# Fourier tables of the convolution made in pieces during the first eight steps, and adaLN sums on VectorE issued at half the rate

## Chip, core and metric

The kernel runs on one core of a Trainium2 chip. The metric is the device time of one execution in microseconds; the median of three runs of the kernel before is 1817.89 us (1816.94 to 1818.36).

A core has five engines that each work through a list of their own, in order: TensorE (PE; its weight loads are PEld), VectorE (DVE), ScalarE (ACT), GpSimd (POOL) and SyncE (SP), which here issues nearly all loads from memory. An instruction that waits holds up everything behind it on its engine.

## What is computed

Two layers over 256 latent tokens with a context prefix of 256 tokens, width 1024. Layer 0 mixes tokens with a Conformer convolution, layer 1 with a bidirectional chunkwise mLSTM; each is followed by a squared-ReLU MLP. Six adaLN vectors for each layer and stream modulate and gate the sub-layers.

```python
for i in range(DEPTH):                                   # DEPTH = 2
    sh1, sc1, g1, sh2, sc2, g2 = adaln(c[:, None, :], ada_w[i], ada_b[i])     # silu(c) @ w + b
    csh1, csc1, cg1, csh2, csc2, cg2 = adaln(c_ctx, ada_w[i], ada_b[i])
    u, uc = modulate(h, sh1, sc1), modulate(hc, csh1, csc1)
    y, yc = conformer_conv(...) if i % 2 == 0 else mlstm_mixer(...)
    h = layer_norm(ALPHA * h + g1 * y, ...)
    h = layer_norm(ALPHA * h + g2 * sq_relu_mlp(modulate(h, sh2, sc2), w1, w2), ...)
    ...                                                  # hc the same, while it is needed

def conformer_conv(u, rows, ...):
    a = u @ w_pw1 + b_pw1
    a = a[..., :CONV_DIM] * sigmoid(a[..., CONV_DIM:])
    a = dwconv(a, w_dw)                                  # 31 taps for each channel
    a = silu(layer_norm(a + b_dw, ln_g, ln_b))
    return a @ w_pw2 + b_pw2
```

## The kernel before

Activations lie with channels on the 128 partitions and the 512 tokens (256 context, 256 latent) along the free axis. Every large product is made in float32 accuracy from three products of rounded parts: `mm3` multiplies the high parts (L177), high with low (L180) and low with high (L181). A weight block comes as a 1 MB load into `raw` (three buffers) and is split by ScalarE into `wh` (L154) and by VectorE into `wl` (L155), four buffers each.

**The first eight steps** (loop over `f`, `start0`, `start1`, `start2`). Step f loads a block of adaLN weights, one of the input and one of the first projection. TensorE makes the adaLN product into the PSUM bank `fl` (L291), VectorE copies it (L603), TensorE folds it (L299, bank `ln`), VectorE adds the bias (L608, L609), ScalarE and VectorE make the modulated input `u` in two parts (L574, L575, L577), and TensorE adds its share to four output blocks of the first projection (`start2`, twelve products of 512 columns). TensorE's products of this loop are held in the order of the program.

**The tables.** The convolution over time is made with Fourier tables of length 128: F0, G1, G2 (transform and back) and WC, WS. VectorE makes them by a cosine polynomial (L654 to L671), which stands behind the eight steps in the program. WC and WS times the 31 taps give the taps' spectrum `Hc`, `Hs` (four products of TensorE at L693 with 31 rows, in float32, read by ScalarE at L694). It is first needed in `spectral` (L762 on), after the projection's eighth output block.

**The adaLN sums on VectorE.** Nine of the adaLN units of layer 1 are not made as products with a thin operand but as sums: `AdaV.step` loads one 256 KB block into `ar` (one buffer, on SP's queue, L353) and adds it times a column to two accumulators of 128x512 (L357 first, L359 after). Eight steps are a unit. Then `rows()` sums over the partitions with a product by ones (L372) into a PSUM tile that ScalarE copies (L374), and after each second unit `end()` transposes the rows (L381) into another tile, to which VectorE adds the bias (L382). `ada_n1` is four units beside the MLP of layer 0, `ada_n2` five more: two are made beside the v projection, and the other three (24 steps) here:

- `queries(h)`, four heads: eight weight blocks of `wq` each, with one `ada_n2.step()` after each block;
- `pair(p)`, two pairs of heads: after the queries of both heads, 16 output blocks m, each with 24 products of 272 columns into the bank `mm`, read by ScalarE and VectorE into `rr` (L154, L155, L1164), and, one block later, 12 products of 512 columns into the four accumulators `acc`, which take the banks `ln`, `ln`, `cv` and `fl`.

PSUM has eight banks: `mm` three, rotating through all large products, `ln` two, `cv` two, `fl` one. `rows()` and `end()` take `fl`, the bank that `acc` takes as well.

The order of each engine's list is made by the framework's scheduler from the program; it is fixed when the kernel is built.

Of the kernel before, what the change touches and what calls it, by code (L numbers as in the profile page):

```python
# [72 lines left out]
def hybrid_kernel(ctx: ExitStack, tc: tile.TileContext, xT, vecs_d, wdw_d, ada0_w, ada_w, wg_d, pw1a, pw1, pw2, w1_0, w2_0,  # L73
# [28 lines left out]
    def psum(tag="mm"):  # L102
        return pp.tile([P, 512], F32, tag=tag, name=nm(tag), bufs={"mm": 3, "ln": 2, "fl": 1, "cv": 2}[tag])
# [237 lines left out]
    class AdaV:  # L341
# [22 lines left out]
                self.end()  # L364

        def rows(self, n):
            ps = psum("fl")
            if n == 0:
                self.sb = tmp("F")
            for s in range(2):  # L370
                j = 32 * (2 * n + s)
                nc.tensor.matmul(ps[j:j + 32, :], ones[:, 0:32], self.acc[s], start=True, stop=True,  # L372
                                 tile_position=(0, j))
            nc.scalar.copy(self.sb[64 * n:64 * n + 64], ps[64 * n:64 * n + 64])  # L374

        def end(self):
            nu, o = self.nu, _OFF[f"ada_b{self.l}"][0] + 4 * self.u0
            r = 64 * nu
            tr = psum("fl")[:, 0:4 * r]
            for b in range(4):  # L380
                nc.tensor.transpose(tr[:, b * r:(b + 1) * r], self.sb[:r, b * P:(b + 1) * P], ident[:r, :r])  # L381
            nc.vector.tensor_tensor(  # L382
                ada[self.l][:, 4 * self.u0:4 * (self.u0 + nu), :].rearrange("p (v b) s -> p b v s", b=4),
                tr.rearrange("p (b v s r) -> p b v s r", b=4, v=nu, s=2)[:, :, :, :, 0],
                vecs[:, o:o + 4 * nu].rearrange("p (v b o) -> p b v o", b=4, o=1).broadcast_to([P, 4, nu, 2]), op=ALU.add)
# [241 lines left out]
    pin[0] = False

    HL = L // 2
    ij = F()
    fj, jj = ij[:, 0:L], ij[:, L:2 * L]
    pc = padp.tile([P, 8], F32, name="pc")
    exact = dict(channel_multiplier=0, allow_small_or_imprecise_dtypes=True)
    nc.gpsimd.iota(fj[:, 0:HL + 1], [[1, HL + 1]], base=0, **exact)
    nc.gpsimd.iota(fj[:, HL + 1:L], [[1, HL - 1]], base=1, **exact)
    nc.gpsimd.iota(jj, [[1, L]], base=0, **exact)
    p_, gt, fp, p15, ph1, ph2, cf, z0 = [pc[:, i:i + 1] for i in range(8)]  # L640
    nc.gpsimd.iota(p_, [[1, 1]], base=0, channel_multiplier=1, allow_small_or_imprecise_dtypes=True)
    nc.vector.tensor_scalar(gt, p_, float(HL), None, op0=ALU.is_gt)
    nc.vector.scalar_tensor_tensor(fp, gt, -float(HL), p_, op0=ALU.mult, op1=ALU.add)
    nc.vector.tensor_scalar(p15, p_, float(NTAP // 2), None, op0=ALU.subtract)
    nc.vector.tensor_scalar(ph1, gt, -L / 4, None, op0=ALU.mult)
    nc.vector.tensor_scalar(ph2, gt, -L / 4, L / 4, op0=ALU.mult, op1=ALU.add)

    nc.vector.tensor_scalar(z0, p_, 0.0, None, op0=ALU.is_equal)
    nc.vector.tensor_scalar(cf, p_, float(HL), None, op0=ALU.is_equal)
    nc.vector.tensor_tensor(cf, cf, z0, op=ALU.add)  # L650
    nc.vector.tensor_scalar(cf, cf, -1.0 / L, 2.0 / L, op0=ALU.mult, op1=ALU.add)
    tab = padp.tile([P, 5 * L], F32, name="tab")
    F0, G1, G2, WC, WS = [tab[:, i * L:(i + 1) * L] for i in range(5)]
    nc.vector.tensor_scalar(F0, fj, p_, None, op0=ALU.mult)  # L654
    nc.vector.tensor_scalar(G1, jj, fp, ph1, op0=ALU.mult, op1=ALU.add)
    nc.vector.tensor_scalar(G2, jj, fp, ph2, op0=ALU.mult, op1=ALU.add)
    nc.vector.tensor_scalar(WC, fj, p15, None, op0=ALU.mult)
    nc.vector.tensor_scalar(WS, fj, p15, -L / 4, op0=ALU.mult, op1=ALU.add)
    nc.vector.tensor_scalar(F0[:, HL + 1:L], F0[:, HL + 1:L], -L / 4, None, op0=ALU.add)
    for t_ in (tab[:, 0:3 * L], tab[:, 3 * L:5 * L]):  # L660
        tz, sq_ = [F()[:, :t_.shape[-1]] for _ in range(2)]
        nc.vector.tensor_scalar(tz, t_, 1.0 / L, MAGIC, op0=ALU.mult, op1=ALU.add)
        nc.vector.tensor_scalar(tz, tz, MAGIC, -float(L), op0=ALU.subtract, op1=ALU.mult)
        nc.vector.tensor_tensor(t_, t_, tz, op=ALU.add)
        nc.vector.scalar_tensor_tensor(tz, t_, -1.0, t_, op0=ALU.mult, op1=ALU.max)
        nc.vector.tensor_scalar(t_, tz, -1.0, L / 4, op0=ALU.mult, op1=ALU.add)
        nc.vector.tensor_tensor(sq_, t_, t_, op=ALU.mult)
        nc.vector.tensor_scalar(tz, sq_, SIN[5], None, op0=ALU.mult)
        for k in (4, 3, 2, 1):
            nc.vector.scalar_tensor_tensor(tz, tz, SIN[k], sq_, op0=ALU.add, op1=ALU.mult)  # L670
        nc.vector.scalar_tensor_tensor(t_, tz, SIN[0], t_, op0=ALU.add, op1=ALU.mult)  # L671

    def masked(name, zero):
        t = padp.tile([P, L], F32, name=name)
# [9 lines left out]
    WIN = [[(F0[0:96, :], 0)], [(ge32, 0), (lt32, 1)], [(ge96, 0), (F0[0:96, :], 1)], [(ge32, 1)]]  # L684
    bdw = padp.tile([P, D], F32, name="bdw")
    nc.sync.dma_start(bdw, wdw_d[NTAP:NTAP + 1, :].broadcast_to([P, D]))
    Hc, Hs = [padp.tile([P, D], F32, name=n_) for n_ in ("Hc", "Hs")]
    for h_ in range(2):
        wd = F()[:NTAP, :]
        nc.sync.dma_start(wd, wdw_d[0:NTAP, h_ * 512:(h_ + 1) * 512])  # L690
        for t, w_ in ((Hc, WC), (Hs, WS)):
            ps = psum("ln")
            nc.tensor.matmul(ps, w_[:NTAP, :], wd, start=True, stop=True)  # L693
            nc.scalar.activation(t[:, h_ * 512:(h_ + 1) * 512], ps, AF.Identity, scale=cf)  # L694


    def gate_w(part, t):
# [421 lines left out]
    def queries(h):  # L1119
        qq = []  # L1120

        def q_epi(m, ps):
            if m < 2:
                flush()
            t = qd.tile([P, 2, QW], F32R, tag="qq", name=nm("qq"), bufs=8)
            split(t[:, 0, :C], t[:, 1, :C], ps)
            split(t[:, 0, C:], t[:, 1, C:], rk[:, 4 * h + m, :])
            qq.append((t[:, 0, :], t[:, 1, :]))

        for _ in gemm_steps(wq, range(2 * h, 2 * h + 2), xcl, C, q_epi, pre=preq):  # L1130
            ada_n2.step()
        return qq

    def pair(p):
        qq = [queries(2 * p + i) for i in range(2)]
        flush()
        acc = [psum(t) for t in ("ln", "ln", "cv", "fl")]
        todo = []

        def scores(n):  # L1140
            while len(todo) > n:
                m, r = todo.pop(0)
# [406 lines left out]
```

## Time and profile before

| | |
|---|---|
| runs, median (lowest to highest) | 1817.89 us (1816.94 to 1818.36) |
| the profiled execution | 1820.06 us |
| its span, first to last instruction | 1818.3 us |
| mean granted clock of TensorE | 0.982 |
| loads of `ar` (256 KB each) | 72, 2.8 us from issue to landing in the median |

The rows of the profile that matter are shown with the prediction. A row of the timeline reads: start in us, duration, engine, line, operation, what is written and from what, its size, how many; in brackets how long the engine stood idle before it, and for whom. Durations of TensorE's products overlap; the distance of two starts is what one costs. A row of the waits reads: who waited at which line, for whom, us in total, times, the longest.

### The profile page before, as it was taken

Reading aid. Unit: us, or ns where it says so; the run is one execution under the profiler, and the core shown is the slowest. Engines: PE = TensorE matmul, PEld = TensorE weight load, DVE = VectorE, ACT = ScalarE, POOL = GpSimd, SP = SyncE. Lnnn points to the kernel's source line nnn. Section 1 sums busy time; section 2 is a strip of 40 time slices with the busy share of each in tenths; the row PEclk is TensorE's granted clock in tenths of the full one; section 3 lists DMA queues with packets and bytes.
Section 4 is the critical chain, followed back from the end, with each engine's and each line's share of the span. In section 5 each row is a group of like instructions: output and inputs, shape, how many; then the busy total and the mean of one; then the engine's idle time right before and its main releaser. Section 6 shows DMA issues by size and latency. Waiting matters only on the chain.

```text
span 1818.3 us, 28103 instructions
## 1 busy us (share of the span) xinstructions
PE 1749.5 (96%) x11410; PEld 1518.2 (83%) x11410; DVE 1111.2 (61%) x2071; ACT 764.6 (42%) x1212; POOL 8.4 (0%) x60
## 2 busy tenths in 40 slices
PE   8999999999999999999999699999999999979996
PEld 5564998888889999876879599988999999859996
DVE  5456996566446978731347453523777667876666
ACT  4311753223233656522335223423858645434443
POOL 0000000000000000000000000000000000000000
PEclk9999999999999999999999799999999999989998
DMA  9424416334322375677547332443535345455551
GB/s 346 151 104 149 158 57 226 129 129 157 112 96 93 108 246 183 190 267 248 186 155 252 141 126 101 163 139 116 186 125 195 122 169 202 163 206 189 186 186 47
DMA packets 67250, 295.65 MB, mean 163 GB/s; under 512 B 6770, under 2 KB 22642, under 8 KB 36144
## 3 DMA queue, kind: packets, MB, share of 16 engines
q1 hardware_dynamic: 49456, 279.16, 44.1%
q10 hardware_dynamic: 17664, 14.69, 2.4%
q8 instruction: 90, 1.47, 0.3%
q14 instruction: 40, 0.33, 0.1%
HBM read 278.09 MB, written 15.73 MB: 162 GB/s over the span
## 4 chain that ended last, share of the span: by engine, by line
PE 88%; DVE 5%; ACT 3%; DMA 2%; issue 1%; SPq 0%; DVEq 0%; ACTq 0%
PE mm L177 25%; PE mm L181 25%; PE mm L180 25%; DVE wl L155 1%; DMA raw<-ada_w 1%; PE fl L291 1%; PE fl L718 1%; PE cv L787 1%; DMA ar<-ada_w 1%; PE ln L177 1%; ACT wh L154 1%; PE ln L181 1%; PE ln L180 1%; PE mm L762 1%; PE fl L372 1%
## 5 line engine op out<-in xcount | busy, mean ns | idle before, releaser
L155 DVE TENSOR_TENSOR wl<-raw,wh 128x1024 fp32r<-128x1024 f32 x354 | 431.0, 1222 | 323.9 <-ACT wh L154 321.1
L154 ACT CAST wh<-raw 128x1024 fp32r<-128x1024 f32 x354 | 368.6, 1050 | 613.4 <-PE mm L180 529.5
L180 PE MATMUL mm<-u,wh 128*128 128x256 f32 (+1 forms) x1400 | 448.2, 320 | 0.0
L177 PE MATMUL mm<-u,wh 128*128 128x256 f32 (+1 forms) x1272 | 398.7, 315 | 7.4 <-ACT u L1456 2.1
L181 PE MATMUL mm<-u,wl 128*128 128x256 f32 (+1 forms) x1272 | 396.9, 313 | 1.1 <-DVE wl L155 1.1
L180 PEld LDWEIGHTS mm<-u,wh 128*128 128x128 f32 x1400 | 268.4, 192 | 19.5 <-issue 1.6
L177 PEld LDWEIGHTS mm<-u,wh 128*128 128x128 f32 x1272 | 243.6, 192 | 30.4 <-ACT wh L154 7.4
L181 PEld LDWEIGHTS mm<-u,wl 128*128 128x128 f32 x1272 | 244.4, 192 | 16.6 <-DVE wl L155 2.3
L177 PE MATMUL mm<-hid,wh 128*128 128x256 f32 (+1 forms) x512 | 166.2, 325 | 0.0
L181 PE MATMUL mm<-hid,wl 128*128 128x256 f32 (+1 forms) x512 | 165.3, 323 | 0.0
L180 PE MATMUL mm<-hid,wh 128*128 128x256 f32 (+1 forms) x512 | 165.3, 323 | 0.0
L177 PE MATMUL mm<-xl,wh 128*128 128x256 f32 x512 | 147.8, 289 | 1.0 <-ACT wh L154 0.8
L180 PE MATMUL mm<-xl,wh 128*128 128x256 f32 x512 | 146.7, 287 | 0.6 <-DVE xl L155 0.6
L181 PE MATMUL mm<-xl,wl 128*128 128x256 f32 x512 | 146.4, 287 | 0.2 <-DVE wl L155 0.2
L359 DVE SCALAR_TENSOR_TENSOR L<-ar,cs,L 128x512 f32<-128x512 f32 x126 | 90.0, 748 | 68.0 <-DMA ar<-ada_w 68.0
L177 PEld LDWEIGHTS mm<-hid,wh 128*128 128x128 f32 x512 | 97.4, 190 | 9.5 <-ACT wh L154 1.7
L181 PEld LDWEIGHTS mm<-hid,wl 128*128 128x128 f32 x512 | 97.4, 190 | 7.6
L180 PEld LDWEIGHTS mm<-hid,wh 128*128 128x128 f32 x512 | 97.4, 190 | 7.6 <-issue 0.2
L177 PE MATMUL mm<-xm,wh 128*128 128x512 f32 x256 | 102.9, 402 | 0.0
L177 PEld LDWEIGHTS mm<-xl,wh 128*128 128x128 f32 x512 | 99.3, 194 | 3.8 <-issue 1.7
L180 PEld LDWEIGHTS mm<-xl,wh 128*128 128x128 f32 x512 | 99.3, 194 | 1.7 <-DVE xl L155 0.8
L181 PE MATMUL mm<-xm,wl 128*128 128x512 f32 x256 | 100.3, 392 | 0.0
(417 smaller groups left out, 3013.6 us busy)
## 6 DMA issues: line engine op xcount, KB each, us to landing
raw<-w SPq DMA_DIRECT2D x64, 1024.0 KB, 4.9
raw<-wo SPq DMA_DIRECT2D x32, 1024.0 KB, 4.9
raw<-ada_w SPq DMA_DIRECT2D x30, 1024.0 KB, 4.9
ar<-ada_w SPq DMA_DIRECT2D x72, 256.0 KB, 2.8
raw<-wv SPq DMA_DIRECT2D x16, 1024.0 KB, 5.6
raw<-wqT SPq DMA_DIRECT2D x16, 1024.0 KB, 5.3
raw<-wq SPq DMA_DIRECT2D x16, 1024.0 KB, 5.4
raw<-wk SPq DMA_DIRECT2D x16, 1024.0 KB, 4.8
```

The lines of the kernel that those rows point to most:

```text
L154: c = nc.scalar.copy(hi, src)
L155: nc.vector.tensor_tensor(lo, src, hi.bitcast(F32), op=ALU.subtract)
L177: a = nc.tensor.matmul(ps, wh, xh, start=start, stop=False)
L180: nc.tensor.matmul(ps, wh, xl, start=False, stop=False)
L181: nc.tensor.matmul(ps, wl, xh, start=False, stop=stop)
L291: a = nc.tensor.matmul(ps[32 * j:32 * j + 32], cs[:, kt, 14 - 2 * v:46 - 2 * v], blocks[kt], start=first and kt < 4, stop=last and kt >= 4 ...
L359: nc.vector.scalar_tensor_tensor(a, w, c, a, op0=ALU.mult, op1=ALU.add)
L372: nc.tensor.matmul(ps[j:j + 32, :], ones[:, 0:32], self.acc[s], start=True, stop=True, tile_position=(0, j))
L718: nc.tensor.matmul(wqs[0][32 * j:32 * j + 32, :], wgp[0][:, kt, :], raw[:, j * 512:(j + 1) * 512], start=kt == 0, stop=kt == ET - 1, tile_ ...
L762: nc.tensor.matmul(xfs[b], fm, A[0:fm.shape[0], t, sl], start=i == 0, stop=i == len(w_) - 1)
L787: return nc.tensor.matmul(o[r:r + 64, :], g_[:, r:r + 64], ps_[b][i], start=i == 0, stop=i == 1, tile_position=(0, r))
```

## The change

Two parts. The tables become a generator of thirteen pieces, `tables()`; each of the first steps calls it twice, between `start0` and `start2`. WC and WS come first and their products with the taps follow at once; the taps are loaded with the first piece; temporaries come from the pools `E` and `L` instead of `F`. And `queries` calls `ada_n2.step()` at each second block only, while each second output block of `pair` calls it once; `rows()` and `end()` take tiles of the bank `mm`, so that `acc` can hold `fl` while the sums run.

```diff
         def rows(self, n):
-            ps = psum("fl")
+            ps = psum()
...
         def end(self):
...
-            tr = psum("fl")[:, 0:4 * r]
+            tr = psum()[:, 0:4 * r]
...
+    def tables():
+        ij = tmp("E")
...
+        wds = []
+        for h_ in range(2):
+            wds.append(tmp("E")[:NTAP, :])
+            nc.sync.dma_start(wds[-1], wdw_d[0:NTAP, h_ * 512:(h_ + 1) * 512])
...
+        def cosine(t_):
+            tz, sq_ = [tmp("L")[:, :t_.shape[-1]] for _ in range(2)]
+            nc.vector.tensor_scalar(tz, t_, 1.0 / L, MAGIC, op0=ALU.mult, op1=ALU.add)
+            nc.vector.tensor_scalar(tz, tz, MAGIC, -float(L), op0=ALU.subtract, op1=ALU.mult)
+            nc.vector.tensor_tensor(t_, t_, tz, op=ALU.add)
+            yield
+            nc.vector.scalar_tensor_tensor(tz, t_, -1.0, t_, op0=ALU.mult, op1=ALU.max)
+            nc.vector.tensor_scalar(t_, tz, -1.0, L / 4, op0=ALU.mult, op1=ALU.add)
+            nc.vector.tensor_tensor(sq_, t_, t_, op=ALU.mult)
+            yield
+            nc.vector.tensor_scalar(tz, sq_, SIN[5], None, op0=ALU.mult)
+            for k in (4, 3, 2, 1):
+                nc.vector.scalar_tensor_tensor(tz, tz, SIN[k], sq_, op0=ALU.add, op1=ALU.mult)
+                if k % 2:
+                    yield
+            nc.vector.scalar_tensor_tensor(t_, tz, SIN[0], t_, op0=ALU.add, op1=ALU.mult)
+
+        nc.vector.tensor_scalar(WC, fj, p15, None, op0=ALU.mult)
+        nc.vector.tensor_scalar(WS, fj, p15, -L / 4, op0=ALU.mult, op1=ALU.add)
+        yield
+        yield from cosine(tab[:, 0:2 * L])
+        for h_ in range(2):
+            for t, w_ in ((Hc, WC), (Hs, WS)):
+                ps = psum("ln")
+                nc.tensor.matmul(ps, w_[:NTAP, :], wds[h_], start=True, stop=True)
+                nc.scalar.activation(t[:, h_ * 512:(h_ + 1) * 512], ps, AF.Identity, scale=cf)
+            yield
...
+        yield from cosine(tab[:, 2 * L:5 * L])
+
+    side = tables()
     pin[0] = Z.pin0
     for f in range(DT + 2):
         if 0 <= f - 1 < DT:
             start1(f - 1)
         if f < DT:
             start0(f)
+        for _ in range(2):
+            next(side, None)
         if f >= 2:
             start2(f - 2)
     pin[0] = False
...
-        for _ in gemm_steps(wq, range(2 * h, 2 * h + 2), xcl, C, q_epi, pre=preq):
-            ada_n2.step()
+        for i, _ in enumerate(gemm_steps(wq, range(2 * h, 2 * h + 2), xcl, C, q_epi, pre=preq)):
+            if i % 2:
+                ada_n2.step()
...
+            if m % 2:
+                ada_n2.step()
             scores(0)
```

Three places in the engines' lists show what moves. Lines are those of each kernel's own file (the spectrum's products are L693 before and L676 after; the `rr` sums L1164 and L1186).

TensorE in the first steps, from the adaLN product of step 2 on. Before:

```order
L291 MATMUL fl_193<-raw_188,cs 32x256 x8
L177 MATMUL mm_113<-u_141,wh_149 128x512
L180 MATMUL mm_113<-u_142,wh_149 128x512
L181 MATMUL mm_113<-u_141,wl_150 128x512
L177 MATMUL mm_114<-u_141,wh_149 128x512
```

And after:

```order
L291 MATMUL fl_228<-raw_223,cs 32x256 x8
L676 MATMUL ln_242<-E_145,tab 128x512
L676 MATMUL ln_245<-E_145,tab 128x512
L177 MATMUL mm_113<-u_170,wh_178 128x512
L180 MATMUL mm_113<-u_171,wh_178 128x512
```

The first half of the spectrum now stands ahead of the first products of the projection; the second half stands in the same way behind the adaLN product of step 3. On VectorE at the same place, between the bias of step 1 and the copy of step 2, before:

```order
L609 TENSOR_SCALAR sc1p<-ln_170,vecs 128x2
L575 TENSOR_SCALAR S_177<-x_153,sc1p,sh1p 128x256 x2
L155 TENSOR_TENSOR wl_184<-F_157,wh_183 128x512
L577 TENSOR_TENSOR u_176<-S_177,u_175 128x512
L603 COPY F_202<-fl_193 128x256
```

And after, up to the last operation that the first half of the spectrum needs (L667, which writes WC and WS into tab):

```order
L609 TENSOR_SCALAR sc1p<-ln_205,vecs 128x2
L664 SCALAR_TENSOR_TENSOR L_160<-L_160,L_161 128x256
L575 TENSOR_SCALAR S_212<-x_182,sc1p,sh1p 128x256
L664 SCALAR_TENSOR_TENSOR L_160<-L_160,L_161 128x256
L575 TENSOR_SCALAR S_212<-x_182,sc1p,sh1p 128x256
L155 TENSOR_TENSOR wl_219<-F_186,wh_218 128x512
L577 TENSOR_TENSOR u_211<-S_212,u_210 128x512
L664 SCALAR_TENSOR_TENSOR L_160<-L_160,L_161 128x256
L680 TENSOR_SCALAR tab<-E_140,pc 128x128
L664 SCALAR_TENSOR_TENSOR L_160<-L_160,L_161 128x256
L603 COPY F_237<-fl_228 128x256
L667 SCALAR_TENSOR_TENSOR tab<-L_160,tab 128x256
```

Five steps of the cosine and one start of another table (L680) now stand among the operations of step 1, all but the last of them ahead of the copy of step 2 (L603) that TensorE's next fold reads.

VectorE in the first blocks of `pair(0)`. Before, the end of the second unit (L_8893, L_8894 are its accumulators):

```order
L359 SCALAR_TENSOR_TENSOR L_8893<-ar_9039,cs,L_8893 128x512
L359 SCALAR_TENSOR_TENSOR L_8894<-ar_9039,cs,L_8894 128x512
L359 SCALAR_TENSOR_TENSOR L_8893<-ar_9071,cs,L_8893 128x512
L359 SCALAR_TENSOR_TENSOR L_8894<-ar_9071,cs,L_8894 128x512
L359 SCALAR_TENSOR_TENSOR L_8893<-ar_9110,cs,L_8893 128x512
L359 SCALAR_TENSOR_TENSOR L_8894<-ar_9110,cs,L_8894 128x512
L359 SCALAR_TENSOR_TENSOR L_8893<-ar_9147,cs,L_8893 128x512
L359 SCALAR_TENSOR_TENSOR L_8894<-ar_9147,cs,L_8894 128x512
L382 TENSOR_TENSOR ada_106<-fl_9155,vecs 128x4x2x2
L357 TENSOR_SCALAR L_10001<-ar_10003,cs 128x512
L357 TENSOR_SCALAR L_10002<-ar_10003,cs 128x512
L155 TENSOR_TENSOR rr_9266<-mm_9267,rr_9265 128x256
```

And after, the same unit under other numbers (L_9199, L_9200), with the splits of the output blocks:

```order
L359 SCALAR_TENSOR_TENSOR L_9199<-ar_9413,cs,L_9199 128x512
L359 SCALAR_TENSOR_TENSOR L_9200<-ar_9413,cs,L_9200 128x512
L155 TENSOR_TENSOR rr_9228<-mm_9229,rr_9227 128x256
L1186 TENSOR_TENSOR wgq<-wgq,mm_9229 128x16
L155 TENSOR_TENSOR rr_9228<-mm_9245,rr_9227 128x256
L1186 TENSOR_TENSOR wgq<-wgq,mm_9245 128x16
L359 SCALAR_TENSOR_TENSOR L_9199<-ar_9519,cs,L_9199 128x512
L359 SCALAR_TENSOR_TENSOR L_9200<-ar_9519,cs,L_9200 128x512
L155 TENSOR_TENSOR wl_9432<-raw_9429,wh_9431 128x1024
L155 TENSOR_TENSOR rr_9274<-mm_9275,rr_9273 128x256
L1186 TENSOR_TENSOR wgq<-wgq,mm_9275 128x16
L155 TENSOR_TENSOR wl_9436<-raw_9429,wh_9435 128x1024
```

Four steps and the first of the next unit stood in one block ahead of the `rr` splits; now one step stands behind the splits of each output block.

TensorE at the end of the second unit of layer 0's MLP stage, before:

```order
L372 MATMUL fl_3416<-L_3118,ones 32x512
L372 MATMUL fl_3416<-L_3119,ones 32x512
L177 MATMUL mm_3432<-hid_3114,wh_3428 128x512
L180 MATMUL mm_3432<-hid_3115,wh_3428 128x512
L181 MATMUL mm_3432<-hid_3114,wl_3429 128x512
L177 MATMUL mm_3437<-hid_3114,wh_3433 128x512
L180 MATMUL mm_3437<-hid_3115,wh_3433 128x512
L181 MATMUL mm_3437<-hid_3114,wl_3434 128x512
L177 MATMUL mm_3432<-hid_3156,wh_3428 128x512
L180 MATMUL mm_3432<-hid_3157,wh_3428 128x512
L181 MATMUL mm_3432<-hid_3156,wl_3429 128x512
L381 MATMUL fl_3420<-ident,F_3074 128x128 x4
```

And after:

```order
L372 MATMUL mm_3416<-L_3118,ones 32x512
L372 MATMUL mm_3416<-L_3119,ones 32x512
L381 MATMUL mm_3420<-ident,F_3074 128x128 x4
L177 MATMUL mm_3432<-hid_3114,wh_3428 128x512
L180 MATMUL mm_3432<-hid_3115,wh_3428 128x512
```

The transposes of `end()` (L381), which read what ScalarE copies from the rows, stood behind nine products and now stand directly behind the rows.

More of the change, by code (lines that the diff above doesn't have):

```diff
@@ L617, in start2 @@
             mm3(ps0[m], *kcol(st[f], m), *u[f], f == 0, f == DT - 1)
+    HL = L // 2
+    pc = padp.tile([P, 8], F32, name="pc")
+    tab = padp.tile([P, 5 * L], F32, name="tab")
+    WC, WS, F0, G1, G2 = [tab[:, i * L:(i + 1) * L] for i in range(5)]
+    Hc, Hs = [padp.tile([P, D], F32, name=n_) for n_ in ("Hc", "Hs")]
+    def tables():
+        ij = tmp("E")
+        fj, jj = ij[:, 0:L], ij[:, L:2 * L]
+        exact = dict(channel_multiplier=0, allow_small_or_imprecise_dtypes=True)
+        nc.gpsimd.iota(fj[:, 0:HL + 1], [[1, HL + 1]], base=0, **exact)
+        nc.gpsimd.iota(fj[:, HL + 1:L], [[1, HL - 1]], base=1, **exact)
+        nc.gpsimd.iota(jj, [[1, L]], base=0, **exact)
+        p_, gt, fp, p15, ph1, ph2, cf, z0 = [pc[:, i:i + 1] for i in range(8)]
+        nc.gpsimd.iota(p_, [[1, 1]], base=0, channel_multiplier=1, allow_small_or_imprecise_dtypes=True)
+        wds = []
+        for h_ in range(2):
+            wds.append(tmp("E")[:NTAP, :])
+            nc.sync.dma_start(wds[-1], wdw_d[0:NTAP, h_ * 512:(h_ + 1) * 512])
+        nc.vector.tensor_scalar(gt, p_, float(HL), None, op0=ALU.is_gt)
+        nc.vector.scalar_tensor_tensor(fp, gt, -float(HL), p_, op0=ALU.mult, op1=ALU.add)
+        nc.vector.tensor_scalar(p15, p_, float(NTAP // 2), None, op0=ALU.subtract)
+        nc.vector.tensor_scalar(ph1, gt, -L / 4, None, op0=ALU.mult)
+        nc.vector.tensor_scalar(ph2, gt, -L / 4, L / 4, op0=ALU.mult, op1=ALU.add)
+        nc.vector.tensor_scalar(z0, p_, 0.0, None, op0=ALU.is_equal)
+        nc.vector.tensor_scalar(cf, p_, float(HL), None, op0=ALU.is_equal)
+        nc.vector.tensor_tensor(cf, cf, z0, op=ALU.add)
+        nc.vector.tensor_scalar(cf, cf, -1.0 / L, 2.0 / L, op0=ALU.mult, op1=ALU.add)
+        def cosine(t_):
[24 more added lines that the diff above has]
+            yield
+        nc.vector.tensor_scalar(F0, fj, p_, None, op0=ALU.mult)
+        nc.vector.tensor_scalar(G1, jj, fp, ph1, op0=ALU.mult, op1=ALU.add)
+        nc.vector.tensor_scalar(G2, jj, fp, ph2, op0=ALU.mult, op1=ALU.add)
+        nc.vector.tensor_scalar(F0[:, HL + 1:L], F0[:, HL + 1:L], -L / 4, None, op0=ALU.add)
+        yield
+        yield from cosine(tab[:, 2 * L:5 * L])
@@ L627, in hybrid_kernel @@
     pin[0] = False
[L632 to L671, printed above, removed]
+    for _ in side:
+        pass
@@ L686, in hybrid_kernel @@
     nc.sync.dma_start(bdw, wdw_d[NTAP:NTAP + 1, :].broadcast_to([P, D]))
[L687 to L694, printed above, removed]
     def gate_w(part, t):
```

## The prediction

> **What bounds the kernel now.** I read the busy table first, then the list of who waited for whom on TensorE, then the windows, and last the timeline around each place where TensorE stood still.
>
> ```profile
> PE 1749.5 (96%) x11410; PEld 1518.2 (83%) x11410; DVE 1111.2 (61%) x2071; ACT 764.6 (42%) x1212; POOL 8.4 (0%) x60
> PE fl L372 <- DVE L L359: 17.0, 1, 17.0
> ```
>
> TensorE is busy 96% of the span, so only its idle time and its time at the low clock can be won. The longest single wait of the whole span is one of 17 us, for VectorE's adaLN sums (L359 is `AdaV.step`, L372 `rows()`). The windows (columns: busy time and instructions of PE, PEld, DVE, ACT and POOL, granted clock, DMA share, GB/s) show where:
>
> ```profile
> 980.00:1000.00 20.00, 19.99 (x163) 19.27 (x163) 15.96 (x25) 8.84 (x15) 0.00 (x0) 1.00 0.69 225
> 1020.00:1040.00 20.00, 4.02 (x25) 3.40 (x23) 6.88 (x9) 1.05 (x1) 0.00 (x0) 0.68 0.28 101
> 1040.00:1060.00 20.00, 18.00 (x89) 13.88 (x90) 8.25 (x21) 3.87 (x9) 0.00 (x0) 0.81 0.27 93
> 1060.00:1080.00 20.00, 20.00 (x125) 18.16 (x124) 13.34 (x28) 6.60 (x12) 0.00 (x0) 1.00 0.45 150
> ```
>
> Beside the queries of heads 0 and 1 (980 to 1000) the sums cost TensorE nothing. In the first blocks of `pair(0)` it stands still, and afterwards, with sums still running (1060 to 1080), it is full again.
>
> **Term 1, the sums at half the rate.** The timeline of that place, VectorE's last step first, then TensorE:
>
> ```profile
> 1040.25 1.41 DVE L359 SCALAR_TENSOR_TENSOR L<-ar,cs,L 128x512 f32<-128x512 f32 x2 [2.73 <-DMA ar<-ada_w]
> 1023.73 0.29 PE L181 MATMUL mm<-qq,wl 128*128 128x272 f32 x1
> 1041.06 2.57 PE L372 MATMUL fl<-L,ones 128*32 128x512 f32 x4 [17.04 <-DVE L L359]
> 1044.30 1.11 PE L381 MATMUL fl<-ident,F 128*128 128x128 f32 x4 [0.67 <-ACT F L374]
> 1045.68 0.79 PE L177 MATMUL fl<-rr,u 128*128 128x512 f32 x1 [0.27 <-DVE ada L382]
> 1047.86 0.39 PE L181 MATMUL fl<-rr,u 128*128 128x512 f32 x1
> 380.49 1.05 PE L372 MATMUL fl<-L,ones 128*32 128x512 f32 x4
> 1150.15 0.39 PE fl L381 x4
> ```
>
> `ar` has one buffer, so a step is 2.73 us of waiting for its load and 1.41 us of work, 4.14 us in all. Before, the last steps of the second unit stand on VectorE as one block (rows in the change section), ahead of the `rr` splits that TensorE needs, and TensorE waits in `rows()`. What this costs: 17.04 idle; `rows()` at the low clock 2.57 against 1.05 in its other place, 1.52; the transposes of `end()` 1.11 against 0.39, 0.72; waits of 0.67 and 0.27; and five products that take 2.18 from 1045.68 to 1047.86 where five at the full distance of 0.23 (48.62 to 48.85, below) take 1.15, so 1.03. Sum **21.3 us**.
>
> After, the list has one step behind each output block of `pair(0)`. Is there room?
>
> ```profile
> 1056.24 0.24 PE ln L177
> 1062.05 0.24 PE ln L177
> ```
>
> These rows of the chain are the same product of two blocks: a block is 5.81 us, longer than the 4.14 of a step. The third unit already ran like this from 1060, one step to a block, with TensorE full, so I take the whole 21.3 as gone. The eight steps of the third unit move to the queries of heads 2 and 3, where before there were none; that is the stage of the 980 to 1000 row with other heads, and there they were hidden. If that cover were missing, each step would cost what it lasts beyond its cover, at most 4.14.
>
> What is given back: with `rows()` and `end()` in the rotating bank `mm`, the transposes L381 stand right behind `rows()` at three places (two in the MLP of layer 0, one after head 3), where before eight or nine products lay between. TensorE then waits for ScalarE's copy:
>
> ```profile
> 381.32 0.59 ACT L900 ACTIVATE E<-mm 128x512 f32<-128x512 f32 x1
> 381.94 0.59 ACT L374 COPY F<-fl 64x512 f32<-64x512 f32 x1
> ```
>
> `rows()` ends at 380.49 + 1.05 = 381.54, the copy at 382.53: 1.05 us with the hand-over, twice; after head 3 nothing but a small cast is queued ahead, so the 0.67 of above. Sum 2.8. Bounds: 0, if the copies come early, and 5, if a weight cast of ScalarE comes between each time. Net of term 1: **-18.5 us**.
>
> **Term 2, the tables.** First what stands there now, TensorE, then ScalarE's reads of the spectrum:
>
> ```profile
> 14.33 1.93 PE L291 MATMUL fl<-raw,cs 128*32 128x256 f32 x16 [0.36 <-DMA raw<-ada_w]
> 16.19 0.80 PE L177 MATMUL mm<-u,wh 128*128 128x512 f32 x1
> 22.38 0.50 PE L177 MATMUL mm<-u,wh 128*128 128x512 f32 x1
> 48.62 0.39 PE L177 MATMUL mm<-u,wh 128*128 128x512 f32 x1
> 48.85 0.39 PE L180 MATMUL mm<-u,wh 128*128 128x512 f32 x1
> 49.82 0.50 PE L177 MATMUL mm<-u,wh 128*128 128x512 f32 x1 [0.58 <-ACT wh L154]
> 52.62 0.47 PE L177 MATMUL mm<-u,wh 128*128 128x512 f32 x1 [2.07 <-DVE E L744]
> 54.99 0.50 PE L181 MATMUL mm<-u,wl 128*128 128x512 f32 x1 [0.67 <-DVE wl L155]
> 58.63 5.01 PE L693 MATMUL ln<-F,tab 31*128 31x512 f32 x8
> 63.58 1.12 PE L747 MATMUL ln<-ident,E 128*128 128x128 f32 x4
> 68.45 0.40 PE L177 MATMUL mm<-u,wh 128*128 128x512 f32 x1
> 59.79 0.69 ACT L694 ACTIVATE Hc<-ln,pc 128x512 f32<-128x512 f32 x1 [8.13 <-PE ln L693]
> 60.65 0.69 ACT L694 ACTIVATE Hs<-ln,pc 128x512 f32<-128x512 f32 x1 [0.17 <-PE ln L693]
> 61.98 0.69 ACT L694 ACTIVATE Hc<-ln,pc 128x512 f32<-128x512 f32 x1 [0.64 <-PE ln L693]
> 63.69 0.69 ACT L694 ACTIVATE Hs<-ln,pc 128x512 f32<-128x512 f32 x1 [1.02 <-PE ln L693]
> ```
>
> Gone: the three waits behind a VectorE full of table work, 3.32; the spectrum's four products at L693, 4.95 (58.63 to 63.58); and the low clock after them: from 63.58 to 68.45 stand eight products and two groups of transposes, worth 8 x 0.23 + 2 x 0.39 = 2.6, in 4.87, so 2.3. Together 10.6.
>
> Added: the same four products, in pairs behind the adaLN products of steps 2 and 3. The last two reads lie 1.71 us apart, the first two 0.86: a product costs 1.7 at the low clock, 0.87 at the full one. The first pair runs while the clock is still low, 3.4; the second 1.74.
>
> The first pair also waits for VectorE. Its list between the copies of steps 0 and 2:
>
> ```profile
> 8.61 0.42 DVE L603 COPY F<-fl 128x256 f32<-128x256 f32 x1 [3.37 <-PE fl L291]
> 12.47 0.42 DVE L603 COPY F<-fl 128x256 f32<-128x256 f32 x1
> 49.25 0.42 DVE L665 SCALAR_TENSOR_TENSOR F<-tab 128x256 f32<-128x256 f32 x1
> 49.58 0.56 DVE L670 SCALAR_TENSOR_TENSOR F<-F,F 128x384 f32<-128x384 f32 x1
> 50.05 0.29 DVE L666 TENSOR_SCALAR tab<-F 128x256 f32<-128x256 f32 x1
> 50.25 0.56 DVE L670 SCALAR_TENSOR_TENSOR F<-F,F 128x384 f32<-128x384 f32 x1
> ```
>
> From start to start a 256-wide two-input operation takes 0.33 and a one-input one 0.20. Behind the copy at 8.61 now come eleven tiny ones (0.9), three 128-wide (0.65), three 256-wide one-input (0.6), two two-input (0.66), and step 0's own work (2.1): 4.9, so the copy of step 1 is at 13.9 instead of 12.47. TensorE's fold and adaLN products then end at about 17.2 instead of 16.26. From the fold's end, 15.4, VectorE needs another 4.65 for step 1's work and the rest of the first cosine: the tables WC and WS are ready at 20.1, the pair runs from 20.1 to 23.5, and the first product of step 0 starts at **23.5 instead of 16.19**: 7.3 later. Less 0.3, since more of step 0 then runs at the full clock, plus 1.74: 8.7. The second cosine lies on VectorE in the time in which TensorE is in that pair and step 0 (5 us of work in 8), (a 384-wide operation takes 0.47 from 49.58 to 50.05, and there are twelve, some of them one-input), so I give it no price; without that cover it costs up to 5. The two loads of taps now go ahead of the second adaLN block on SP's queue; 124 KB beside 1.5 MB a step, nothing to see.
>
> Term 2: -10.6 + 8.7 = **-1.9 us**; bounds -5.8 (the pair need not wait) and +8 (cosine in the way, pair later by 5).
>
> The clock in the first stage fell in the middle of L693 (read distances 0.86, then 1.71) and came back at 68.45. [...]
>
> **Sum.** -18.5 - 1.9 = -20.4 on the profiled execution's 1820.06 us (span 1818.3 and 1.76 around it), 1799.7. That execution is 2.17 above the median of 1817.89, so I predict **1797.5 us**.
>
> **Rivals.** (a) The tables cost more than they free: VectorE's list is the bottleneck of the first 35 us and term 2 is at its upper bound, +8: 1817.9 - 18.5 + 8 = 1807.4. For it: in this stage TensorE and VectorE hand work to each other within each step, so what is put on one delays the other. Against: steps 3 to 7 have nothing added. (b) The stall does not go but is halved, because the third unit, now beside the queries of heads 2 and 3, holds up the splits there: 10.6 lost, 1808.1. Against: the 980 to 1000 row. (c) Slower: SP's queue.
>
> ```profile
> SPq L353 <- DMA ar<-ada_w: 119.9, 44, 6.6
> ```
>
> The longest wait of that kind is 6.6; if loads of `wk` and `wq` made it the rule, a step would last 6.6 + 1.41 = 8.0 us against a block of 5.81, and fifteen steps in line would cost 33 us, 1830. It decides from 7.2 us a step. The step at 1040.25 and the full window at 1060 speak against it. (d) The change does not do what it says: the list shows one step to a block, not to two, so the rate is what VectorE's order makes it; that leaves the forecast as it is. (e) The first pair needs no wait: term 2 at -5.8, 1793.6.
>
> **How the numbers follow.** Forecast 0.62, (a) 0.20, (b) 0.08, (c) 0.03, (e) 0.07. The range reaches from 1790 (e with free transposes) to 1808.5, which takes in (a) and (b). A difference below 0.2% (3.6 us) can't be told from no change. Faster 0.95; the same 0.03, if (a) and (b) come together; slower 0.02.
>
> **What would show it.** Right: no TensorE wait over 2 us near L372; window 1020 to 1040 full; `rows()` followed by about 1 us of idle at three places; TensorE idle near 3 us ahead of the first spectrum pair, the first product near 23.5; no low clock from 61 to 68. Wrong: waits for `wl` or `rr` beside the queries of heads 2 and 3, a low clock beyond step 1, or the first product after 27.

## Result and the profile after

The changed kernel takes **1804.99 us** (median of 4 runs, 1802.84 to 1806.92) against 1818.12 (4 runs, 1816.94 to 1819.11): a ratio of 0.9928, 95% interval 0.9911 to 0.9945 (ratios are of the means of the runs). It is faster by 13.1 us. The forecast was 20.4 us faster, 1797.5, with a range of 1790 to 1808.5: right in sign and in its main mechanism, too large by 7.5 us. The profiled execution took 1805.32 us (span 1803.6), 14.74 less than that of before.

The busy table of after, then its list of who waited for whom on TensorE (us in total, times, longest):

```profile
PE 1743.1 (97%) x11410; PEld 1515.4 (84%) x11410; DVE 1111.6 (62%) x2071; ACT 763.0 (42%) x1212; POOL 8.8 (0%) x60
```

```profile
PE fl L291 <- DMA raw<-ada_w: 20.3, 7, 6.8
PE mm L381 <- ACT F L374: 2.8, 3, 1.0
PE ln L676 <- DVE tab L667: 2.5, 1, 2.5
```

The 17 us wait at L372 is gone. The three waits at L381 are there with the 2.8 us that were forecast, and the first spectrum pair waits 2.5 us for VectorE's tables. The first row was not forecast: TensorE waits 20.3 us for adaLN blocks from memory. The same row of before:

```profile
PE fl L291 <- DMA raw<-ada_w: 10.2, 6, 6.6
```

The windows of after where TensorE stood still before, and the one behind head 3 with its new L381 wait:

```profile
1020.00:1040.00 20.00, 20.00 (x123) 18.03 (x123) 12.44 (x26) 5.77 (x12) 0.00 (x0) 1.00 0.52 181
1040.00:1060.00 20.00, 20.00 (x128) 18.27 (x127) 11.53 (x22) 6.24 (x11) 0.00 (x0) 1.00 0.32 103
1140.00:1160.00 20.00, 19.22 (x156) 18.11 (x155) 10.90 (x19) 8.53 (x15) 0.00 (x0) 1.00 0.54 180
```

4.02 and 18.00 us of work have become 20.00 and 20.00, at the full clock. Now the start, TensorE's timeline of after:

```profile
16.69 1.94 PE L291 MATMUL fl<-raw,cs 128*32 128x256 f32 x16 [6.80 <-DMA raw<-ada_w]
24.93 3.78 PE L676 MATMUL ln<-E,tab 31*128 31x512 f32 x4 [2.53 <-DVE tab L667]
28.64 0.80 PE L177 MATMUL mm<-u,wh 128*128 128x512 f32 x1
34.57 1.98 PE L676 MATMUL ln<-E,tab 31*128 31x512 f32 x4
```

Step 1's adaLN products start at 16.69. The same row of before:

```profile
10.48 1.94 PE L291 MATMUL fl<-raw,cs 128*32 128x256 f32 x16 [0.37 <-DMA raw<-ada_w]
```

Everything behind these products is late: the first product of step 0 is at 28.64 where 23.5 was forecast, beyond the 27 that the prediction named as a sign of a wrong step.

To see stage by stage where the time went, the same four ScalarE instructions are looked up in both timelines: the convolution's first sigmoid, a copy of the normalization behind layer 0's MLP, the copy of the gates behind all heads, and a ReLU of the last MLP. Before, then after:

```profile
179.30 0.57 ACT L848 ACTIVATE S<-ln,vecs 128x256 f32<-128x256 f32 x1 [25.04 <-PE ln L845]
574.35 0.38 ACT L447 COPY ln<-ln 128x256 f32<-128x256 f32 x1 [11.71 <-PE ln L446]
1267.80 0.59 ACT L1201 COPY L<-cv 128x512 f32<-128x512 f32 x1 [3.49 <-PE cv L1051]
1631.36 0.40 ACT L900 ACTIVATE E<-cv 128x256 f32<-128x256 f32 x1
```

```profile
183.46 0.56 ACT L869 ACTIVATE S<-ln,vecs 128x256 f32<-128x256 f32 x1 [26.71 <-PE ln L866]
580.39 0.37 ACT L447 COPY ln<-ln 128x256 f32<-128x256 f32 x1 [11.71 <-PE ln L446]
1252.39 0.59 ACT L1225 COPY L<-cv 128x512 f32<-128x512 f32 x1 [3.49 <-PE cv L1072]
1616.62 0.40 ACT L921 ACTIVATE E<-cv 128x256 f32<-128x256 f32 x1
```

After stands at +4.16, +6.04, -15.41 and -14.74 against before. The differences between neighbours are what each stage gained or lost. The table has them for after and, by the same four rows of their timelines, for the first four experiments:

| stage (by the clock of before) | forecast | after | e1 | e2 | e3 | e4 |
|---|---|---|---|---|---|---|
| start and convolution, to 179 | -1.9 | +4.16 | -2.02 | -3.59 | +5.81 | -6.99 |
| layer 0's MLP, to 574 (two L381 waits) | +2.1 | +1.88 | +1.85 | +2.13 | -0.15 | +1.61 |
| projections and heads, to 1268 | -20.6 | -21.45 | -21.42 | -21.41 | +2.90 | -20.88 |
| rest, to 1631 | 0 | +0.67 | -1.15 | -1.32 | -1.04 | -1.29 |

Term 1 came out as forecast, within 1.1 us. The miss is in the first row, 6.1 us.

### The profile page after: what moved, and what is told of

It reads as the page before. It is cut to its first block, busy times and chain, and to the rows that moved or that the text cites. A ratio compares the mean times of both kernels' runs of the same rounds, so it can differ in the third digit from the quotient of the medians.

```text
span 1803.6 us, 28105 instructions
## 1 busy us (share of the span) xinstructions
PE 1743.1 (97%) x11410; PEld 1515.4 (84%) x11410; DVE 1111.6 (62%) x2071; ACT 763.0 (42%) x1212; POOL 8.8 (0%) x60
## 4 chain that ended last, share of the span: by engine, by line
PE 88%; DVE 5%; ACT 3%; DMA 2%; issue 1%; SPq 0%; ACTq 0%; DVEq 0%
PE mm L177 25%; PE mm L181 25%; PE mm L180 25%; DMA raw<-ada_w 2%; DVE wl L155 1%; PE fl L291 1%; ACT wh L154 1%; PE cv L808 1%; PE fl L739 1%; PE ln L177 1%; PE ln L181 1%; PE ln L180 1%; PE cv L181 1%; PE mm L783 1%; PE cv L180 1%
## 5 line engine op out<-in xcount | busy, mean ns | idle before, releaser
L177 PE MATMUL mm<-u,wh 128*128 128x256 f32 (+1 forms) x1272 | 397.8, 314 | 4.7 <-ACT u L1480 2.1
L177 PEld LDWEIGHTS mm<-u,wh 128*128 128x128 f32 x1272 | 243.3, 192 | 27.1 <-issue 5.1
L177 PE MATMUL mm<-hid,wh 128*128 128x256 f32 (+1 forms) x512 | 166.0, 324 | 0.0
L177 PE MATMUL mm<-xl,wh 128*128 128x256 f32 x512 | 147.8, 289 | 1.0 <-ACT wh L154 0.8
L177 PEld LDWEIGHTS mm<-hid,wh 128*128 128x128 f32 x512 | 97.4, 190 | 7.9 <-issue 0.2
L177 PE MATMUL mm<-xm,wh 128*128 128x512 f32 x256 | 102.9, 402 | 0.0
L177 PEld LDWEIGHTS mm<-xl,wh 128*128 128x128 f32 x512 | 99.3, 194 | 3.8 <-issue 1.7
```

Of the source, the lines that this page charges most:

```text
L177: a = nc.tensor.matmul(ps, wh, xh, start=start, stop=False)
```

## Experiments

Three of the ten runs ask what delays step 1's block, two take the parts of the change singly, four look for a better version, one repeats the changed kernel. Medians are compared with runs of the kernel before on the same chip.

**e1: 32 rows instead of 31.** In the timeline of SyncE of after, the two loads of taps stand ahead of step 1's block:

```profile
2.66 0.90 SPq L640 DMA_DIRECT2D E<-wdw_d  x2
3.61 0.50 SPq L150 DMA_DIRECT2D raw<-ada_w  x1
...
11.05 0.33 SPq L150 DMA_DIRECT2D raw<-ada_w  x1
14.28 0.33 SPq L596 DMA_DIRECT2D x<-xT  x1
```

```profile
SPq L150 <- DMA E<-wdw_d: 3.0, 1, 3.0
SPq L596 <- DMA E<-wdw_d: 2.9, 1, 2.9
```

The block is issued at 3.61, only 1 us later than before (2.66), so the issue is not what makes it 6 us late. But SyncE's own waits show that the two small loads land only near 11.05 and 14.28, 3.23 us apart: 62 KB in 31 rows, 0.104 us a row, so 6.4 us for the 62 rows of both. That these rows hold up the block was the author's estimate; e1 gives each load one row more.

```diff
-            wds.append(tmp("E")[:NTAP, :])
-            nc.sync.dma_start(wds[-1], wdw_d[0:NTAP, h_ * 512:(h_ + 1) * 512])
+            wds.append(tmp("E")[:NTAP + 1, :])
+            nc.sync.dma_start(wds[-1], wdw_d[0:NTAP + 1, h_ * 512:(h_ + 1) * 512])
...
-                nc.tensor.matmul(ps, w_[:NTAP, :], wds[h_], start=True, stop=True)
+                nc.tensor.matmul(ps, w_[:NTAP, :], wds[h_][:NTAP, :], start=True, stop=True)
```

> The changed kernel with one edit: each load of taps takes 32 rows of the array instead of 31 (one row of biases more, which no product reads), at the same place in SP's list. [...] Then step 1's adaLN products start near 10.7 us instead of 16.69, the first product of step 0 near 23.5 instead of 28.64, and the time is about 5 us less, 1800. Theory B: it is the place ahead of step 1's block and the bytes that cost, or VectorE's list that sets the start: step 1's products stay at 16 to 17 and the time at 1805 within 1.5.

Measured: 1798.47 us (1797.40 to 1801.80), ratio 0.9890 (0.9876 to 0.9903), 6.5 us less than the changed kernel. TensorE's timeline of e1:

```profile
11.34 1.93 PE L291 MATMUL fl<-raw,cs 128*32 128x256 f32 x16 [1.32 <-DMA raw<-ada_w]
19.87 3.78 PE L676 MATMUL ln<-E,tab 31*128 31x512 f32 x4 [2.81 <-DVE tab L667]
23.58 0.80 PE L177 MATMUL mm<-u,wh 128*128 128x512 f32 x1
```

Theory B is out: with the same instructions on every engine in the same order and 4 KB more to load, the block's products start 5.35 us sooner, and the first product stands at 23.58, the forecast's 23.5. VectorE's list and the place of the loads are not the cause of the late block.

**e5: half the dose.** Only the first of the two loads takes 32 rows. If each 31-row load adds to the delay, the block's products start near 14 and the first product near 26, between e1 and after; if not, they start at 11.3 or at 16.7 as in those two.

```diff
-            wds.append(tmp("E")[:NTAP, :])
-            nc.sync.dma_start(wds[-1], wdw_d[0:NTAP, h_ * 512:(h_ + 1) * 512])
+            n_ = NTAP + 1 - h_
+            wds.append(tmp("E")[:n_, :])
+            nc.sync.dma_start(wds[-1], wdw_d[0:n_, h_ * 512:(h_ + 1) * 512])
```

> The changed kernel with only one of the two loads of taps on 32 rows, the other on 31, at the same place. [...]

Measured: 1801.17 us (1800.02 to 1802.52), ratio 0.9898 (0.9881 to 0.9915). The timeline of e5:

```profile
13.70 1.93 PE L291 MATMUL fl<-raw,cs 128*32 128x256 f32 x16 [3.59 <-DMA raw<-ada_w]
25.64 0.80 PE L177 MATMUL mm<-u,wh 128*128 128x512 f32 x1
```

With none, one and two loads of 31 rows the block's products start at 11.34, 13.70 and 16.69, and the medians are 1798.5, 1801.2 and 1805.0: the delay follows the dose.

The traces hold a more direct sign: the times of the landing signals that they record for each load. Each 31-row load of after has two, one just behind its issue and one at its end (3.22 and 10.96, 3.73 and 14.26); each 32-row load of e1 has sixteen (7.46 to 8.61 and 7.78 to 8.93). Step 1's block has sixteen in each of these traces. In after fifteen of them come from 9.93 to 10.66 and the last at 16.55; in e5 fifteen come by 11.36 and the last at 13.56; in e1 all sixteen come by 11.20. So in after one of the block's sixteen signals was late, by 16.55 - 11.20 = 5.35 us against e1, and in all three traces TensorE's products start 0.14 us behind the last one (16.69, 13.70, 11.34).

**e6: the 31-row loads at another place.** The pieces of the tables are handed out from step 2 on (e4 below), with the old loads.

```diff
-        for _ in range(2):
+        for _ in range(2 if f >= 2 else 0):
             next(side, None)
```

> As e4 (pieces from step 2 on), but with the 31-row loads. They now stand behind step 2's loads and ahead of step 3's adaLN block. Theory A: that block lands about 6.4 us late, near 24 to 25 where e4 ran its products at 20.96, so TensorE waits 3 to 4 us there and the time is 1798 to 1799. Theory B: with more loads in flight by then nothing is delayed, 1795.

Measured: 1798.29 us (1792.70 to 1801.98), ratio 0.9882 (0.9863 to 0.9902). The timeline of e6:

```profile
24.11 1.93 PE L291 MATMUL fl<-raw,cs 128*32 128x256 f32 x16 [2.58 <-DMA raw<-ada_w]
```

Now it is step 3's block that is late: 24.11 instead of 20.96 in e4 (the row is under e4). The delay moves with the loads, as theory A says; the time lies where it expected, though these runs scatter by 9 us.

**e2: the sums alone.** The kernel before with only the rate of the steps and the banks of `rows()` and `end()` changed.

```diff
-            ps = psum("fl")
+            ps = psum()
...
-            tr = psum("fl")[:, 0:4 * r]
+            tr = psum()[:, 0:4 * r]
...
-        for _ in gemm_steps(wq, range(2 * h, 2 * h + 2), xcl, C, q_epi, pre=preq):
-            ada_n2.step()
+        for i, _ in enumerate(gemm_steps(wq, range(2 * h, 2 * h + 2), xcl, C, q_epi, pre=preq)):
+            if i % 2:
+                ada_n2.step()
...
+            if m % 2:
+                ada_n2.step()
             scores(0)
```

> The kernel before with the second half of the change alone (sums at half the rate, rows() and end() in the rotating bank). Theory A (places matched between the two traces): the sums are worth about 22.5 less 3.1 given back, 19.4 in all, so 1798.7 us, below the changed kernel's 1805. Theory B: the tables gained 1.9 as forecast and the sums fell short: 1818.1 - 11.2 = 1806.9.

Measured: 1798.62 us (1795.84 to 1799.54), ratio 0.9889 (0.9874 to 0.9904): 20.3 us less than the 1818.96 beside it. Theory A.

**e3: the tables alone.** The changed kernel with the four edits of e2 taken back.

```diff
-            ps = psum()
+            ps = psum("fl")
...
-            if m % 2:
-                ada_n2.step()
             scores(0)
```

> The changed kernel without the sums part: only the tables and the spectrum are spread over the first steps. Theory A: this part costs 2.5 us up to the first windowed products, 4 if the clock also falls near 180 us, so 1820.6 to 1822. Theory B (the forecast's term): 1.9 us faster than before, 1816.2.

Measured: 1825.22 us (1824.14 to 1827.56), ratio 1.0037 (1.0025 to 1.0050), so 6.3 us slower than before. The direction is theory A's, the size above its 1820.6 to 1822. The list of waits and the windows of e3:

```profile
PE fl L291 <- DMA raw<-ada_w: 20.0, 8, 6.8
PE fl L372 <- DVE L L359: 18.6, 2, 17.1
```

```profile
170.00:180.00 10.00, 7.34 (x36) 1.63 (x36) 9.67 (x43) 0.00 (x0) 0.00 (x0) 0.86 0.58 217
180.00:190.00 10.00, 9.35 (x45) 2.88 (x45) 4.72 (x19) 3.67 (x8) 0.00 (x0) 0.80 0.63 229
```

Two things were not in the expectation: a second wait at L372 of 18.6 - 17.1 = 1.5 us, and a low clock near 180 for (0.14 + 0.20) x 10 / 0.5 = 6.8 us instead of 3.4. The two parts add up: -20.3 and +6.3 on 1818.96 give 1805.0, the changed kernel's time.

**e4: tables from step 2, with 32 rows.** The edit of e6 and that of e1 together.

> The changed kernel with the 32-row loads, and the pieces of the tables handed out from step 2 on instead of step 0. Theory A: VectorE and the loads have room once TensorE is full, so the first product of step 0 is back near 16.2, the spectrum's four products cost about 0.43 each at the full clock (1.7), and no wait remains behind the tables: about 11 us less than the changed kernel, 1794. Theory C: two pieces of VectorE's work a step delay each of six steps by about 1.3 us, since a step hands work between TensorE and VectorE: 1800 to 1802.

Measured: 1794.87 us (1792.50 to 1796.58), ratio 0.9866 (0.9852 to 0.9879), 10.1 us less than the changed kernel. The timeline of e4:

```profile
15.95 0.79 PE L177 MATMUL mm<-u,wh 128*128 128x512 f32 x1
20.96 1.07 PE L291 MATMUL fl<-raw,cs 128*32 128x256 f32 x16
...
25.52 1.12 PE L676 MATMUL ln<-E,tab 31*128 31x512 f32 x2
26.57 1.07 PE L291 MATMUL fl<-raw,cs 128*32 128x256 f32 x16
28.16 1.12 PE L676 MATMUL ln<-E,tab 31*128 31x512 f32 x2 [0.52 <-DVE sc1p L609]
```

The first product is back at 15.95. Two points of the expectation were wrong: a spectrum product takes 1.05 (25.52 to 26.57), not 0.43, so the four cost 4.2 us, and one wait for VectorE remains, 0.5 us. The rest of theory A holds.

**e7: `end()` one step later.** e4, with the transposes of `end()` put off so that products lie between `rows()` and them.

```diff
-            if self.i == DT * self.nu:
-                self.end()
...
         def step(self):
+            self.drain()
             if self.todo:
                 a = self.todo[0]
                 a.step()
                 if a.i == DT * a.nu:
-                    self.todo.pop(0)
+                    self.pend = self.todo.pop(0)
+
+        pend = None
+
+        def drain(self):
+            if self.pend is not None:
+                self.pend.end()
+                self.pend = None
...
             if not cab1:
+                ada_n1.drain()
                 cab1.extend(comb(1, "ln2_g0", "ln2_b0", "sc1", "sh1"))
...
     for p in range(2):
         pair(p)
+    ada_n2.drain()
```

> e4 with the transposes of end() put off to the next step of the sums, so that products lie between rows() and them again. Theory A: the three waits of 2.8 us in all behind ScalarE's copy go and nothing takes their place: e4's 1794.9 less 2.8, 1792.1. Theory B: the wait was cover for something else, such as the copies of ScalarE that come late anyway: within 1 us of e4.

Measured: 1795.04 us (1791.94 to 1795.51), ratio 0.9857 (0.9837 to 0.9877), no better than e4, though no wait at L381 is left in its list. The timeline of e7 behind the MLP:

```profile
614.53 0.39 PE L177 MATMUL mm<-u,wh 128*128 128x256 f32 x1 [1.48 <-DVE E L1030]
654.04 0.39 PE L177 MATMUL mm<-u,wh 128*128 128x256 f32 x1 [1.81 <-DVE E L1030]
```

By the row at 574.35 e7 has gained 2.6 us on e4 (-7.99 against -5.38); by the same kind of row at 740.97 it has lost them and more (-3.68 against -5.40). In e4 the first of these waits is 1.4 us long and the second isn't there. Behind the second one e7 also runs 3.4 us at half clock, from 654.34 on, which costs it another 1.7 us. The steps of this stage were used up, so the last unit's transposes came only when the normalization asked for them: in TensorE's list 580 rows behind `rows()`, where the other units have about 50.

**e9 and e10: the same, mended, beside e4 once more.** The last unit's transposes come at the MLP's next block.

```diff
         if c < 2:
             ada_n1.step()
+        else:
+            ada_n1.drain()
```

> e7 mended: the transposes of the last unit of the MLP's sums now come at the next block of the MLP (50 products behind rows(), as the others) and not, as in e7, only when the MLP's normalization asks for them. Theory A: in e7 the late transposes and the VectorE work behind them stood in the way of the stage behind the MLP, where the 2.6 us that had been gained were lost again; mended, the three waits stay away and the time is e4's less 2.8, near 1792. Theory B: the loss in e7 has another cause: the waits of TensorE for VectorE's E near 614 and 654 us are there again, and the time is that of e4 and e7, 1795.

> e4 once more, on the same chip as e9 for the comparison: 1794.9 within 1.5 us.

Measured: e9 1790.75 us (1788.84 to 1793.06), ratio 0.9849 (0.9834 to 0.9863); e10, the unchanged e4, 1794.89 (1791.70 to 1797.55), ratio 0.9865 (0.9848 to 0.9882). e9's list has no L381 wait and its products at L177 wait only once for VectorE's `E`, for 1.4 us, so theory A stands and e7's loss came from the late transposes. The two ratios' intervals overlap: that the waits are gone is shown, that e9 is 2.8 us faster than e4 isn't resolved. Against the kernel before and against the changed one e9 is the fastest version here.

**e8: the changed kernel again.** The prediction assumed no new stretch of low clock. After has one, behind a wait that is as long as in before:

```profile
177.62 1.05 PE L291 MATMUL fl<-raw,cs 128*32 128x512 f32 x2 [2.77 <-DMA raw<-ada_w]
```

```profile
170.00:180.00 10.00, 7.16 (x36) 1.64 (x36) 9.25 (x41) 0.00 (x0) 0.00 (x0) 0.95 0.65 242
180.00:190.00 10.00, 9.35 (x56) 4.09 (x52) 6.03 (x23) 4.86 (x11) 0.00 (x0) 0.88 0.74 274
```

(0.05 + 0.12) x 10 / 0.5 = 3.4 us at half clock. In before the matching row waits 2.75 us, for VectorE, and the clock stays at 1.00:

```profile
175.10 1.04 PE L291 MATMUL fl<-raw,cs 128*32 128x512 f32 x2 [2.75 <-DVE mv L525]
```

> The changed kernel itself once more, for a second trace. Theory A: whether TensorE gets a stretch of 3.4 us at half clock near 180, 1258 and 1313 us is a matter of the execution (where its idle time falls against a window of the clock's), not of the kernel: some of the three are gone in this trace while the waits there are the same, and the profiled time differs by about 1.7 us for each. Theory B: the late landing of the block at 177.62 causes the first one: it is there again.

Measured: 1806.56 us (2 runs), ratio 0.9928 (0.9900 to 0.9955), profiled 1807.10. The windows of e8:

```profile
170.00:180.00 10.00, 7.14 (x34) 1.54 (x32) 9.66 (x42) 0.00 (x0) 0.00 (x0) 0.88 0.56 208
180.00:190.00 10.00, 9.35 (x42) 2.64 (x42) 4.46 (x17) 3.32 (x8) 0.00 (x0) 0.77 0.61 229
```

The stretch is there again and twice as long, (0.12 + 0.23) x 10 / 0.5 = 7 us, as theory B says. But e4 and e10 are one kernel too, and they differ. The windows of e4, then of e10:

```profile
20.00:40.00 20.00, 19.48 (x128) 11.98 (x127) 15.54 (x41) 7.94 (x15) 1.80 (x8) 1.00 0.84 327
170.00:180.00 10.00, 9.35 (x65) 4.24 (x61) 7.27 (x28) 5.85 (x14) 0.00 (x0) 1.00 0.90 314
```

```profile
20.00:40.00 20.00, 19.05 (x98) 11.41 (x98) 14.53 (x37) 7.45 (x13) 1.75 (x8) 0.83 0.84 333
170.00:180.00 10.00, 8.49 (x38) 2.38 (x40) 5.98 (x24) 2.35 (x5) 0.00 (x0) 0.83 0.75 294
```

0.17 x 20 / 0.5 = 6.8 us and 3.4 us at half clock in e10, none in these windows of e4, and the profiled times are 1797.55 and 1792.50. So such stretches do come and go between executions of one kernel.

What sets the traces apart near 180 can be read from their clock records. In before the granted clock changes sixteen times, first at 20.28, 61.24 and 68.07 us, in after fourteen times, first at 32.18, 178.95 and 182.36; in each of the two all these times lie whole multiples of 3.4133 us apart, to within 0.02 us. Divide both traces at that spacing: in after 2.08 of the 2.77 us of idle time ahead of 177.62 fall into one interval, at whose end, 178.95, the half clock begins; in before the 2.75 us fall into two, 1.53 and 1.22, and the clock stays full. Every one of the twelve traces has the wait of 2.6 to 3.0 us in this stage. Divided in the same way, five have 1.76 us of it or more in one interval (after and e8 2.08, e3 1.76, e9 2.03, e10 2.54), and the half clock begins at the end of that interval. The other seven have at most 1.67 us of it in any (before 1.53, e1 1.45, e2 1.50, e4 1.67, e5 and e6 1.51, e7 1.65), and the clock stays full. It is the place of the wait, theory A's reason, that separates these traces; the 31-row loads aren't needed, since e9 and e10 load 32 rows. No run moved the wait alone, so this was read from twelve traces and not shown by an experiment.

## Why the prediction was right, and where it was not

- **Term 1, the stall (-21.3).** Right. The stage from 574 to 1268 gained 21.4 us in after, e1 and e2, with the L381 wait behind head 3 in it, against 20.6 forecast. One step to a block left TensorE full, and the third unit's steps beside heads 2 and 3 cost nothing: no wait at L372 is left. Rivals (b) and (c) are out. What rival (d) read from the list is so in the trace: the second unit's steps run one to an output block in the first half of `pair(0)`, from 1014.41 to 1051.69, and the second half has none.
- **What is given back (2.8).** Right to the digit: three waits, 2.8 us. e9 shows that they can go without another wait in their place.
- **The wait of the first spectrum pair and the first product at 23.5.** Right in e1 (wait 2.81, product at 23.58), where the loads of taps have 32 rows. Rival (e) is out by the same waits, 2.53 us in after and 2.81 in e1. The second pair took 1.91 (34.57 to the product at 36.48) against 1.74. The 0.3 us that step 0 was to gain from a full clock did not come in e1: its products took 5.13 us (23.58 to 28.71) against 4.76 before (16.19 to 20.95). A low clock beyond step 1, one of the prediction's signs of a wrong step, came neither in after, whose clock records have 1.00 from 32.18 to 178.95, nor in e1; in e10, whose spectrum products stand singly, it came from 28.37 on, in e4 not. The second cosine cost nothing, as forecast: the steps behind it last 4.29 us (39.38 to 43.67), as before (4.33, 25.23 to 29.56).
- **The step that failed**, and with it most of the 7.5 us, is one sentence of term 2: that the two loads of taps ahead of the second adaLN block are "124 KB beside 1.5 MB a step, nothing to see". It was reckoned in bytes. e1, e5 and e6 show that the number of rows counts: with two loads of 31 rows the last of the sixteen signals of the block behind them, and so the products that need it, came 5.35 us later than with 32 rows, and the whole kernel took 6.5 more. The first product comes 28.64 - 23.58 = 5.06 late; 0.6 of it comes back, since step 0's products then take 4.5 instead of 5.1 us, and the stretch of low clock near 180 adds about 1.7.
- **The low clock counted as gone (2.3).** Not a property of the kernel. Windows of before and of e2, which has the same instructions in this stage:

```profile
60.00:80.00 20.00, 20.00 (x75) 14.47 (x74) 3.42 (x4) 8.31 (x12) 0.00 (x0) 0.83 0.35 131
```

```profile
60.00:80.00 20.00, 19.99 (x90) 15.37 (x90) 4.42 (x4) 8.20 (x12) 0.00 (x0) 1.00 0.35 128
```

  Behind the same spectrum products the clock fell in one execution and not in the other. The predicted sign, no low clock from 61 to 68, came true in after (1.00 there), but e2 has it without the tables' move. Without this gain term 2 is worth about nothing, as e1 and e2 agree: 1798.47 with the tables spread and 32 rows, 1798.62 with the tables of before. In the first row of the table, where neither has a low stretch behind the first 30 us, e1 is 1.6 us behind e2.
- **Rival (a)** had the right sign for term 2 and nearly its size (+8 forecast, +6.3 in e3), but VectorE's list, its reason, isn't the cause: e1 has that list and the forecast's start. The measured 1805.0 lies nearer to its 1807.4 than to the forecast's 1797.5; it lies in the range because the range was drawn to take in (a). The argument against it, that steps 3 to 7 have nothing added, was not quite right either: in after the last operations of the second cosine stand behind VectorE's copy of step 3 (35.18) and end at 37.86.
- **The sum by medians:** -20.3 (e2) instead of -18.5, and +6.3 (e3) instead of -1.9.

## What to carry to other kernels

Price a load by its rows as well as by its bytes: here two loads of 31 rows held up the block behind them by 5.35 us, and one row more in each cured it. Filler work belongs where the engine that it shares has slack: the same pieces handed out from the third step on instead of the first were worth another 3.6 us by the medians of e1 and e4. A stretch of low clock seen in a single trace should not be booked as a gain; look whether the idle time ahead of it (2.77 us in after) goes.

## What the runs showed of the hardware

- In after two loads of 31 rows of 2 KB landed 3.23 us apart, 0.104 us a row, while large loads ran beside them. The products that need the 1 MB block behind them started at 11.34 with no such load (e1), at 13.70 with one (e5) and at 16.69 with two (after), so 2.4 to 3.0 us later for each. A 31-row load gave two landing signals where a 32-row load gave sixteen, and the last of the block's own sixteen came at 11.20, 13.56 and 16.55. Why 31 rows do this was not shown.
- The stretches of low clock that the windows above give last 3.4 or 6.8 to 7 us, and an idle time of 2.77 us was followed by one in after, one of 2.75 us by none in before. All changes of the clock lie whole multiples of 3.4133 us apart in before and in after, to within 0.02 us. Divided at that spacing, the traces in which the clock fell near 180 have 1.76 us of idle time or more in one interval there, the others at most 1.67. That is read from twelve traces, and no run tested it by itself.
- A product of 31 rows in plain float32 takes 1.05 us of TensorE at the full clock where the next instruction waits for nothing (25.52 to 26.57 in e4), and 0.96 in the second pair of after (1.91 for two), against 0.23 for a 128-row product of the split weights. The two differ in the number format as well as in the rows, and no run separates these; the fewer rows did not make the product cheap.
